# A zero-fill ahead of ScalarE's first transfer, and a ninth warm-up product, at the start of a hybrid encoder block

## The chip, the core and the metric

The kernel runs on one core of one Trainium2 chip. The metric is the device time of the whole program in microseconds, taken as the median of several runs. The core has a matrix engine (TensorE, called PE in the profile), three engines that work on tiles (VectorE or DVE, ScalarE or ACT, GpSimd or POOL) and SyncE (SP), which here only issues transfers. All transfers run on the same 16 DMA engines, whichever engine issues them.

## The reference, cut to what matters

One encoder block on 256 tokens of width 2048 in float32. What the change touches is only the very beginning, the first norm and the first projection:

```python
u = rmsnorm(h, norm_mix_g[l])
z = u @ w_in[l]
b_a, c_a, v_a, q, k, v, gl_a, gl_b = jnp.split(z, SPLIT_POINTS, axis=-1)
```

After it come a short gated convolution, a windowed attention, two gates, a mixing product, a second norm, a wide feed-forward pair of products with a convolution, and a last norm.

## The kernel before

**How a product is made.** Activations lie transposed, with the width on the partitions in 16 chunks (KT) of 128 rows and the 256 tokens in the columns. Every float32 product is split in two: the weight tile has a high part (`whi`, made by a cast on ACT, L175) and a low part (`wlo`, weight minus high part, on DVE, L186), and the activation tile holds its high and low part side by side in 512 columns (`xs`). One "pair" on PE is then a product of `whi` with 512 columns (L214) and one of `wlo` with 256 columns (L215). The whole program is a stream of such pairs, drawn from the list `chunks` in `run`. Three helpers run ahead of PE for each chunk: `fetch` issues the transfer, `high` makes `whi`, `low` makes `wlo`. All of it is emitted in an order written out by hand, and each engine works through its own instructions in that order.

**The first sixteen chunks.** They are "wide": chunk k holds row block k of the activations x (256 columns) beside row block k of six weight tiles (768 columns), and gives six pairs, one for each of the six jobs in `first`. For them `fetch`, `high` and `low` call `pre_x` at stages 0 to 3. `pre_x` also makes `xs` for chunk k from x and the norm's weight: for k below 3 both parts on DVE (L343 high, L344 low), later the high part on ACT (L336); and it squares x on ACT (L340).

**Chunk 0 is loaded differently.** The arrays for chunk 0 and the x of chunk 1 lie in one array `head`. Two transfers fetch it: SP's first (L319) brings the tile `hd`, 264 KB (the norm's weight, x of chunk 0, and weight blocks 0 and 1), and ACT's first (L320) brings the tile `hb`, 384 KB (weight blocks 2 to 5 of chunk 0, and x of chunk 1). SP then goes on with the wide transfers of chunks 1 to 15 (L326) on its own queue: the first is 384 KB, since its x came with `hb`, and the others are 512 KB. For chunks 0 to 2 the parts are made in two pieces, blocks 0 and 1 and then blocks 2 to 5 (`pieces`), so pairs 0 and 1 of chunk 0 rest on `hd` alone and pairs 2 to 5 on `hb`; chunk 1's `xs` rests on `hb` too.

**Before all that.** DVE fills `ones` (L302) and `eps` (L303), and PE multiplies `ones` by `ones` eight times into a bank that nobody reads (L308, `warm`). ACT's instructions begin with the issue of `hb`'s transfer; the load of its function table comes next, and then the casts.

Of the kernel before, what the change touches and what calls it, by code (L numbers as in the profile page):

```python
# [51 lines left out]
def hybrid_block_kernel(ctx: ExitStack, tc: tile.TileContext, head, wide, xT, w_in, w_oa, w_o, w_mix, w_up, w_dn, vec, cst, out):  # L52
    nc = tc.nc
# [245 lines left out]
    hb = p1.tile([P, WIDE, P], F32, tag="hb", name="hb")  # L299


    nc.vector.memset(ones, 1.0 / D)  # L302
    nc.vector.memset(eps, EPS)  # L303
    xs = cpool.tile([P, KT, 2 * T], F32R, tag="A", name="xs")

    warm = aps.tile([P, 2 * T], F32, tag="tp", name="warm")
    for _ in range(8):
        nc.tensor.matmul(warm[:, 0:P], ones, ones, start=True, stop=True)  # L308
    sq1 = cpool.tile([P, KT, T], F32, tag="B", name="sq1")

# [560 lines left out]
```

## Time and profile before

| what | us |
|---|---|
| median of 3 runs | 1334.39 (1333.92 to 1334.44) |
| the profiled execution, its own time | 1334.16 |
| span of its trace, first to last instruction | 1332.4 |
| PE busy in it | 1321.9 |
| PE's first pair starts at | 5.55 |

All times in the rows below are counted from the start of the span. A line of the timeline gives start, busy time, engine, line of the kernel, operation, and the tile written and read; the bracket at its end gives the idle time of the engine before it and what ended it. ACTq and SPq are the moments at which these engines issue a transfer. PEld is the loading of weights, which overlaps the products. One float32 product of `warm` shows as two records.

### The profile page before, as it was taken

The page shows a single profiled execution, that of the slowest core. Times are in us where ns is not written, and L with a number is a line of the kernel's source. Part 1 is how long each engine was busy: PE and PEld are TensorE (multiplying, and loading weights), DVE is VectorE, ACT ScalarE, POOL GpSimd, SP SyncE. Part 2 cuts the span into 40 slices and gives each one's busy share as a digit, 9 for nine tenths or more (in the row PEclk, how much of TensorE's full clock was granted, in tenths as well). Part 3 has the DMA queues.
Part 4 walks back from the last instruction along what each step waited for, and adds up shares of the span by engine and source line. Part 5 has one row for each costly group of instructions (what it writes and reads, how often), then busy time and mean ns, then how long its engine had stood idle before and what let it go on. Part 6 is the DMA issues. An engine that isn't in the chain of part 4 may idle for free.

```text
span 1332.4 us, 20489 instructions
## 1 busy us (share of the span) xinstructions
PE 1321.9 (99%) x7691; PEld 1162.7 (87%) x7691; DVE 955.4 (72%) x1507; ACT 722.4 (54%) x1151; POOL 71.1 (5%) x66
## 2 busy tenths in 40 slices
PE   9999999999999999999999999999999999999997
PEld 8888888888888888888888888888888888888886
DVE  6988777655557887668888888888888865445444
ACT  7666675555555545446555555555555544444442
POOL 0000000000000003330000000000000001111211
PEclk9999999999999999999999999999999999999999
DMA  8786545555555546547555555555555557666663
GB/s 289 245 240 203 205 159 168 180 190 189 191 190 190 190 145 235 191 139 239 190 189 190 190 190 190 190 190 190 190 189 191 174 151 234 195 187 181 197 192 103
DMA packets 76676, 255.54 MB, mean 192 GB/s; under 512 B 8864, under 2 KB 9248, under 8 KB 76576
## 3 DMA queue, kind: packets, MB, share of 16 engines
q1 hardware_dynamic: 76144, 253.44, 58.5%
q8 instruction: 60, 0.98, 0.3%
q10 hardware_dynamic: 432, 0.79, 0.2%
q14 instruction: 40, 0.33, 0.1%
HBM read 248.16 MB, written 2.10 MB: 188 GB/s over the span
## 4 chain that ended last, share of the span: by engine, by line
PE 99%; DVE 0%; DMA 0%; ACT 0%; POOLq 0%; issue 0%; DVEq 0%; ACTq 0%
PE ps L214 63%; PE ps L215 33%; PE av L490 1%; PE ptp L477 1%; PE s L447 0%; PE s L448 0%; DMA hd<-in_head_dram 0%; PE more L693 0%; POOLq L866 0%; DVE y L735 0%; DVE r L727 0%; DVE x L700 0%; ACT whi L175 0%; PE nps L258 0%; ACT ln L717 0%
## 5 line engine op out<-in xcount | busy, mean ns | idle before, releaser
L186 DVE TENSOR_TENSOR wlo<-raw,whi 128x1024 fp32r<-128x1024 f32 (+3 forms) x493 | 567.7, 1153 | 316.6 <-PE ps L215 223.4
L175 ACT CAST whi<-raw 128x1024 fp32r<-128x1024 f32 (+3 forms) x493 | 488.3, 992 | 328.5 <-PE ps L214 189.9
L214 PE MATMUL ps<-hs,whi 128*128 128x512 f32 x1408 | 488.4, 391 | 0.0
L215 PE MATMUL ps<-hs,wlo 128*128 128x256 f32 x1408 | 393.6, 280 | 0.0
L214 PE MATMUL ps<-xs,whi 128*128 128x512 f32 x1088 | 377.5, 395 | 0.7 <-ACT whi L175 0.7
L214 PEld LDWEIGHTS ps<-hs,whi 128*128 128x128 f32 x1408 | 263.1, 187 | 57.6
L215 PE MATMUL ps<-xs,wlo 128*128 128x256 f32 x1088 | 295.9, 281 | 0.0
L215 PEld LDWEIGHTS ps<-hs,wlo 128*128 128x128 f32 x1408 | 266.1, 189 | 0.4
L214 PEld LDWEIGHTS ps<-xs,whi 128*128 128x128 f32 x1088 | 200.7, 188 | 41.8 <-ACT whi L175 1.0
L215 PEld LDWEIGHTS ps<-xs,wlo 128*128 128x128 f32 x1088 | 206.4, 190 | 5.5
L244 ACT COPY evb<-ps 128x256 f32<-128x256 f32 x188 | 69.7, 372 | 199.3 <-PE ps L215 192.4
L214 PE MATMUL ps<-actC,whi 128*128 128x512 f32 x420 | 146.2, 391 | 0.0
L215 PE MATMUL ps<-actC,wlo 128*128 128x256 f32 x448 | 124.4, 280 | 0.0
L214 PEld LDWEIGHTS ps<-actC,whi 128*128 128x128 f32 x420 | 78.5, 187 | 17.2
L214 PE MATMUL ps<-ms,whi 128*128 128x512 f32 x256 | 88.8, 391 | 0.0
L214 PE MATMUL ps<-ya_att,whi 128*128 128x512 f32 x256 | 88.8, 391 | 0.0
L215 PEld LDWEIGHTS ps<-actC,wlo 128*128 128x128 f32 x448 | 84.8, 189 | 0.0
L214 PE MATMUL ps<-actA,whi 128*128 128x512 f32 x240 | 83.8, 391 | 0.0
L248 DVE TENSOR_TENSOR evt<-ps,evb 128x256 f32<-128x256 f32 x178 | 74.5, 418 | 0.7 <-ACT evb L244 0.7
L215 PE MATMUL ps<-ya_att,wlo 128*128 128x256 f32 x256 | 71.7, 280 | 0.0
L215 PE MATMUL ps<-ms,wlo 128*128 128x256 f32 x256 | 71.7, 280 | 0.0
L215 PE MATMUL ps<-actA,wlo 128*128 128x256 f32 x256 | 70.9, 280 | 0.0
(143 smaller groups left out, 1049.8 us busy)
## 6 DMA issues: line engine op xcount, KB each, us to landing
raw<-in_w_up_dram SPq DMA_DIRECT2D x170, 512.0 KB, 3.8
raw<-in_w_in_dram SPq DMA_DIRECT2D x124, 512.0 KB, 3.8
raw<-in_w_dn_dram SPq DMA_DIRECT2D x70, 512.0 KB, 4.3
raw<-in_w_mix_dram SPq DMA_DIRECT2D x26, 512.0 KB, 3.7
raw<-in_w_dn_dram SPq DMA_DIRECT2D x36, 256.0 KB, 2.7
raw<-in_w_oa_dram SPq DMA_DIRECT2D x16, 512.0 KB, 3.3
raw<-in_w_o_dram SPq DMA_DIRECT2D x16, 512.0 KB, 3.4
raw<-in_wide_dram SPq DMA_DIRECT2D x14, 512.0 KB, 5.4
```

The source lines that it names most:

```text
L175: nc.scalar.copy(his[c][:, a:b, :], raws[c](a, b))
L186: nc.vector.tensor_tensor(los[c][:, a:b, :], raw(a, b), his[c][:, a:b, :], op=ALU.subtract)
L214: lambda: nc.tensor.matmul(both, hi[:, i, :], moving, start=k == 0, stop=last and turned),
L215: lambda: nc.tensor.matmul(ps[:, 0:T], lo[:, i, :], a[:, 0:T], start=False, stop=last and not turned),
L244: nc.scalar.copy(b, ps[:, T : 2 * T])
L248: nc.vector.tensor_tensor(dst, ps[:, 0:T], b, op=ALU.add)
L477: nc.tensor.transpose(tp[:, b, n * P : (n + 1) * P], p[:, n, b * P : (b + 1) * P], ident)
L490: nc.tensor.matmul(o[64 * e : 64 * e + 64, 0:T], vtok[:, b, v0 : v0 + HD], pT[e][:, b, :], start=b == 0, stop=b == 1)
```

## The change

DVE fills the tile `hb` with zeros, after `ones` and `eps`. ACT's transfer into `hb` (L320) writes the same tile later in the program's order, so it now waits for that fill. The loop of warm-up products runs nine times rather than eight. Nothing else is edited.

```diff
     nc.vector.memset(ones, 1.0 / D)
     nc.vector.memset(eps, EPS)
+
+    nc.vector.memset(hb, 0.0)
     xs = cpool.tile([P, KT, 2 * T], F32R, tag="A", name="xs")
 
     warm = aps.tile([P, 2 * T], F32, tag="tp", name="warm")
-    for _ in range(8):
+    for _ in range(9):
         nc.tensor.matmul(warm[:, 0:P], ones, ones, start=True, stop=True)
```

`hb` is 128 partitions by 768 float32 elements.

## Rows read from the trace of the kernel before

**Rows 1.** The page: the span, the busy time of each engine with its share of the span, and the shares of the engines in the chain that ended last.

```profile
span 1332.4 us, 20489 instructions
...
PE 1321.9 (99%) x7691; PEld 1162.7 (87%) x7691; DVE 955.4 (72%) x1507; ACT 722.4 (54%) x1151; POOL 71.1 (5%) x66
...
PE 99%; DVE 0%; DMA 0%; ACT 0%; POOLq 0%; issue 0%; DVEq 0%; ACTq 0%
```

**Rows 2.** The waits of PE over the whole span: who waited for whom, us in total, times, longest.

```profile
PE warm L308 <- DVE eps L303: 1.1, 1, 1.1
PE nps L715 <- ACT sq L714: 1.0, 1, 1.0
PE ps L214 <- ACT whi L175: 0.7, 1, 0.7
```

**Rows 3.** The timeline of PE alone, from the start of the span.

```profile
1.05 3.79 PE L308 MATMUL warm<-ones 128*128 128x128 f32 x16 [1.05 <-DVE eps L303]
5.55 0.76 PE L214 MATMUL ps<-xs,whi 128*128 128x512 f32 x1 [0.72 <-ACT whi L175]
6.12 0.41 PE L215 MATMUL ps<-xs,wlo 128*128 128x256 f32 x1
6.33 0.63 PE L214 MATMUL ps<-xs,whi 128*128 128x512 f32 x1
...
6.97 0.63 PE L214 MATMUL ps<-xs,whi 128*128 128x512 f32 x1
7.40 0.41 PE L215 MATMUL ps<-xs,wlo 128*128 128x256 f32 x1
...
9.53 0.54 PE L214 MATMUL ps<-xs,whi 128*128 128x512 f32 x1
...
10.02 0.39 PE L214 MATMUL ps<-xs,whi 128*128 128x512 f32 x1
...
11.43 0.40 PE L214 MATMUL ps<-xs,whi 128*128 128x512 f32 x1
...
11.79 0.40 PE L214 MATMUL ps<-xs,whi 128*128 128x512 f32 x1
```

**Rows 4.** The timeline of all engines in the same stretch: the first issues of ACT and SP, and the work of ACT and DVE up to chunk 2.

```profile
0.73 0.41 ACTq L320 DMA_DIRECT2D hb<-in_head_dram  x1
0.74 0.38 SPq L319 DMA_DIRECT2D hd<-in_head_dram  x1
0.83 0.17 DVE L302 MEMSET ones<- 128x128 f32 x1 [0.83 <-PEq L860]
0.95 0.06 DVE L303 MEMSET eps<- 128x1 f32 x1
...
1.17 1.28 ACT L175 ACT_TABLE_LOAD   x1 [1.17 <-PEq L860]
...
4.54 0.41 ACT L175 CAST whi<-hd 128x256 fp32r<-128x256 f32 x1 [2.08 <-DMA hd<-in_head_dram]
4.54 0.35 DVE L343 TENSOR_SCALAR xs<-hd 128x256 fp32r<-128x256 f32 x1 [3.53 <-DMA hd<-in_head_dram]
4.85 0.61 ACT L175 CAST whi<-hb 128x512 fp32r<-128x512 f32 x1
4.92 0.48 DVE L344 SCALAR_TENSOR_TENSOR xs<-hd,xs 128x256 fp32r<-128x256 f32 x1
...
5.66 0.68 DVE L186 TENSOR_TENSOR wlo<-hb,whi 128x512 fp32r<-128x512 f32 x1
5.69 0.93 ACT L175 CAST whi<-raw 128x256 fp32r<-128x256 f32 x2 [0.23 <-DMA raw<-in_wide_dram]
...
7.51 0.93 ACT L175 CAST whi<-raw 128x256 fp32r<-128x256 f32 x2 [0.57 <-DMA raw<-in_wide_dram]
...
8.78 1.02 DVE L186 TENSOR_TENSOR wlo<-raw,whi 128x256 fp32r<-128x256 f32 x2
...
10.11 0.95 DVE L186 TENSOR_TENSOR wlo<-raw,whi 128x768 fp32r<-128x768 f32 x1
```

**Rows 5.** The transfers by line over the span: engine that issues, times, KB each, median us from issue to landing.

```profile
raw<-in_w_up_dram SPq DMA_DIRECT2D x12, 256.0 KB, 2.6
...
hb<-in_head_dram ACTq DMA_DIRECT2D x1, 384.0 KB, 4.0
raw<-in_wide_dram SPq DMA_DIRECT2D x1, 384.0 KB, 4.5
hd<-in_head_dram SPq DMA_DIRECT2D x1, 264.0 KB, 3.8
```

**Rows 6.** Windows: start and end, length, busy time and count of PE, PEld, DVE, ACT and POOL, the PEclk column, the mean busy share of the 16 DMA engines, and GB/s moved.

```profile
1.70:2.50 0.80, 0.80 (x6) 0.80 (x5) 0.00 (x0) 0.76 (x1) 0.00 (x0) 1.00 0.81 177
2.50:3.00 0.50, 0.50 (x4) 0.50 (x4) 0.00 (x0) 0.00 (x0) 0.00 (x0) 1.00 0.96 349
3.00:4.00 1.00, 1.00 (x7) 1.00 (x7) 0.00 (x0) 0.00 (x0) 0.00 (x0) 1.00 1.02 384
4.00:5.00 1.00, 0.84 (x4) 0.54 (x3) 0.43 (x2) 0.47 (x2) 0.00 (x0) 1.00 0.99 363
```

**Rows 7.** Groups of DVE's instructions in the first 40 us, different shapes kept apart: count, busy us and mean ns of one.

```profile
L186 DVE TENSOR_TENSOR wlo<-raw,whi 128x768 fp32r<-128x768 f32 x13 | 12.4, 958 | 6.5 <-ACT xs L336 4.9 <-issue 1.0 <-PE ps L215 0.6
...
L186 DVE TENSOR_TENSOR wlo<-raw,whi 128x256 fp32r<-128x256 f32 x2 | 0.8, 419 | 0.0
```

## The prediction

> **What bounds the kernel now.** Read the page first: PE is busy for 1321.9 of 1332.4 us, and the chain that ended last is PE for 99% [rows 1]. Then PE's waits: in the whole span it waits three times, 1.1 us before the first warm-up product, 0.7 us before the first pair and 1.0 us in the finale [rows 2]; what is left of the 10.5 us in which PE is not busy lies after its last product. So nothing but PE's own stream matters, and an edit at the start can give back only what the start loses. Third, PE's timeline from 0 [rows 3]: warm-up from 1.05 to 4.84, idle for 0.72, first pair at 5.55. The pairs then come 0.64 us apart (6.33, 6.97, up to 9.53), and from 10.02 on 0.353 apart ((11.43 - 10.02)/4). A pair is 768 columns, and 768 in 0.64 us is 1.2 a ns: the early pairs run at the clock's lower level, 1.2 GHz, the later ones near the upper. The PEclk column says 1.00 in the early windows too [rows 6], so it holds no reading there and the pace is what is to be trusted. From 9.53 to 10.02 is 0.49; x us at the slow pace and the rest at the fast one make one pair if x/0.64 + (0.49 - x)/0.353 = 1, so x = 0.31: the clock rises at 9.84. **The start loses two things**: 5.5 us before the first pair, and 0.29 us (0.64 - 0.353) on each of some seven slow pairs. My marker for the sum is the start of chunk 2's first pair, 11.79 [rows 3], after which the stream is gapless at the fast pace.
>
> **What sets 5.55.** `hd` is issued at 0.74 and lands after 3.8 us, so at 4.51; then come the cast of its weights and the two parts of its x (DVE 4.54 and 4.92, the second done at 5.40), and PE starts [rows 4, 5]. PE's wait is put down to a cast, but the cast of `hb` ends at 5.46 and the low part of x at 5.40, too near to tell them apart by that view; the code decides, since pairs 0 and 1 use `hd` alone. From landing to first pair are 1.04 us. `hb` is issued at the same moment and lands at 4.73.
>
> **The change, step by step.**
>
> *The fill.* `ones`, 128 elements a partition, takes 0.165 us, and `eps`, one element, 0.06 [rows 4]: (0.165 - 0.06)/127 is 0.83 ns an element. DVE's subtractions give (958 - 419)/512 = 1.05 ns [rows 7]. The fill of 768 elements is then 0.165 plus 640 times either, 0.70 to 0.84 us; I take 0.8, from 1.0 to 1.8. DVE has nothing to do until `hd` lands, so this time costs nothing on DVE itself.
>
> *ACT's wait.* `hb` goes out at about 1.84 (PE started 0.04 after `eps` ended), 1.1 later than now. Queued behind it on ACT is the table load (1.28 us from 1.17), which moves to about 2.27 and ends at 3.55. The first cast needs it; I put `hd`'s landing at 3.5, so the cover is just used up, at a cost of 0.05 for a cast that is not the last thing awaited. SP's queue has no wait added.
>
> *`hd` alone.* Between 1.7 and 3.0 the 16 engines move 0.14 + 0.17 MB, between 3 and 4 another 0.38 [rows 6]. `hd` is 0.27 MB: with nothing beside it, it is through at about 2.9, not 4. The landing is told later than the bytes: `hb` and `hd` together, 0.66 MB, are through at 3.9 and land by 4.73; I allow 0.6 to 0.8 and take 3.5. Bounds: 3.34 (a 256 KB transfer lands 2.6 us after its issue [rows 5]) and 4.51, no gain. The wide transfers on SP's queue stay behind `hd`, as now.
>
> *`hb` late.* By the time it moves, chunk 1's 384 KB is under way too. 264 + 384 + 384 KB are 1.06 MB, which the windows of rows 6 reach at 5.0; landing at 5.6 by the same allowance. Bounds: 1.84 + 3.2 = 5.05 (between the 256 KB row's 2.6 and `hb`'s own 4.0 in company) and 1.84 + 4.5 = 6.3 (chunk 1's 384 KB behind others [rows 5]). I take 5.6, the value from the bytes. Its cast (0.61) ends at 6.24, the subtraction `wlo<-hb` (0.68) then at 6.94, and pair 2's low product can start at 6.99. Now it starts at 7.40 [rows 3].
>
> *The ninth product.* Sixteen records take 3.79 us, the last one overlapping; two more make 0.43. PE is free for a pair at 4.63 now and at 5.06 then. With `hd` at 3.5 the first pair could start at 4.54, so PE starts at **5.06** and the idle 0.72 is gone. Seen alone, the ninth product costs 0.43 of the gain of 0.92 on the start.
>
> *The sum, with the clock left aside.* Pairs at 5.06 and 5.70, pair 2's high product at 6.34 (its cast is done at 6.24), its low product due at 6.77 but ready at 6.99: a stall of 0.22. Pair 3 at 7.20. At the slow pace chunk 0 then ends at 7.20 + 3 x 0.64 = 9.12. If the clock rises at 9.84 as now, 1.12 pairs of chunk 1 are done slowly and 4.88 fast: 9.84 + 1.72 = 11.56 against 11.79, a gain of 0.23.
>
> *The clock.* What the engine did before it rose: it ran without a gap from 5.55 to 9.84, idled 0.72 before that, and had worked from 1.05 to 4.84 with no rise [rows 3]. With the change the idle stretch is gone, work goes on from 1.05, and only the stall of 0.22 near 6.8 breaks it. I expect the rise between 5.06 and 9.84 and take the middle, 7.4. Then pair 3 is 0.31 done at 7.4, the 2.69 pairs left of chunk 0 take 0.95, chunk 1 takes 6 x 0.353 = 2.12, and chunk 2 starts at **10.47, a gain of 1.3**. Any rise earlier than 7.2 gives little more, because `hb` gates pair 2: at best pair 3 at 7.11 and chunk 2 at 10.29, a gain of 1.5.
>
> *What is late next.* DVE's whole backlog moves with `wlo<-hb`, from 5.66 to 6.26, by 0.6: chunk 2's subtractions (8.78, 1.02 long) end at 10.4, chunk 3's (10.11, 0.95 long) at 11.7 [rows 4]; PE wants them from 10.5 and 12.6 on, so they hold, with 0.1 to spare for chunk 2, in which the second piece is needed two pairs later. ACT's casts of chunk 2 wait for a transfer at 7.51 both ways, since the bytes ahead of it are the same.
>
> The profiled execution took 1334.16, 1.8 outside its span, and lies 0.23 under the median. 1334.16 - 1.3 + 0.23 gives 1333.1.
>
> **The rivals.**
>
> *The clock does not follow the gap.* The rise stays where it was and the gain is the 0.23 above: 1334.2. For it: the rise came 4.3 us after the idle stretch ended, and no row shows what PE would have got without it. Against it: 3.79 us of unbroken work, then idle time, then 4.29 us of unbroken work, and only in the last a rise. The Trainium skill ("TensorE: Matmul & The Clock Gate", Part 1: The HAM clock gate) says that the monitor runs freely and does not begin with the kernel, so that the number of slow products differs between runs of one kernel. By that rule the gain would scatter between runs; that the three runs lie within 0.52 us speaks for less scatter than that.
>
> *`hb` comes too late, and the kernel is slower.* The place is pair 2. The point from which it decides: its low product starts 1.39 after `hb` lands (0.03 + 0.61 + 0.02 + 0.68 + 0.05), which is later than today's 7.40 if `hb` lands after 6.0. At the bound of 6.3, pair 2's high product waits from 6.34 to 7.0 and its low one starts at 7.69. That idle time is as long as today's and ends 2.14 later; if the rise moves with it, to 11.98, chunk 0 ends at 9.82, 3.4 pairs of chunk 1 are slow and 2.6 fast, and chunk 2 starts at 12.9: 1.1 slower, 1335.5. For it: chunk 1's 384 KB took 4.5 us, and the engines are full from 2.5 on (0.96 to 1.02 [rows 6]). The Trainium skill ("DMA: Bandwidth & Descriptors", Issuing engines are not separate DMA queues) speaks against the change in the same way: transfers of both queues share the 16 engines, so what `hd` gains `hb` loses. Against it: only one transfer's bytes, not three, lie in `hb`'s way.
>
> *The head's load is not faster.* If `hd` alone lands at 4.51 still, pair 0 starts at 5.55 as now, `hb`'s lateness is hidden (pair 2's low product is due at 7.26), and nothing changes: 1334.4. For it: the first packets need time whatever else runs (177 GB/s up to 2.5). Against it: the byte count and the 256 KB row.
>
> **How the numbers follow.** Forecast 0.58 (1332.3 to 1333.6: from `hb` at its early bound, a gain of 2.05, to a rise not before 8.2), the clock unmoved 0.23, no faster head 0.07, slower 0.12. The range takes in the first three and the noise of runs: 1332.2 to 1334.8. A measurement of this kernel can tell about 0.2%, 2.7 us, from no change. No case reaches that: the largest gain is 2.05 and the largest loss 1.1. What is left for either side is what no row shows: faster 0.03, slower 0.02, the same 0.95.
>
> **What would show it.** In the profile after: a MEMSET of `hb` of 0.7 to 0.84 us on DVE; ACT's issue near 1.84 and the table load near 2.27; the first cast near 3.55; warm-up with 18 records to 5.27; the first pair near 5.06 with no idle time before it; a short wait of PE for `wlo<-hb` near 6.8; 0.353 between pairs well before 9.8; and the start of chunk 2 near 10.5. The prediction is wrong in its main step if the pairs still come 0.64 apart up to about 9.5, and wrong in sign if PE waits for `hb` past 7.4.

## The result, and the profile after

The changed kernel takes **1338.14 us** (median of 9 runs, 1336.76 to 1339.57) against 1333.92 for the kernel before (9 runs, 1332.38 to 1334.46): a ratio of 1.0037, 95% interval 1.0028 to 1.0045. It is slower, by more than the 2.7 us that the prediction called the least a measurement can tell. The profiled execution took 1337.80 with a span of 1336.0, against 1334.16 and 1332.4 before.

The first place to look is PE's waits. Before, 0.7 us stood ahead of the first pair [rows 2]; now there is one wait of 4.1:

```profile
PE ps L214 <- ACT whi L175: 4.1, 1, 4.1
```

PE's timeline tells where it lies. It answers to [rows 3]:

```profile
1.05 3.62 PE L310 MATMUL warm<-ones 128*128 128x128 f32 x18 [1.05 <-DVE ones L302]
4.50 0.47 PE L214 MATMUL ps<-xs,whi 128*128 128x512 f32 x1
...
5.19 0.28 PE L215 MATMUL ps<-xs,wlo 128*128 128x256 f32 x1
9.57 0.80 PE L214 MATMUL ps<-xs,whi 128*128 128x512 f32 x1 [4.10 <-ACT whi L175]
10.30 0.58 PE L215 MATMUL ps<-xs,wlo 128*128 128x256 f32 x1
10.68 0.63 PE L214 MATMUL ps<-xs,whi 128*128 128x512 f32 x1
...
11.32 0.63 PE L214 MATMUL ps<-xs,whi 128*128 128x512 f32 x1
...
14.35 0.39 PE L214 MATMUL ps<-xs,whi 128*128 128x512 f32 x1
...
15.41 0.40 PE L214 MATMUL ps<-xs,whi 128*128 128x512 f32 x1
```

The first pair starts a whole microsecond earlier (4.50 against 5.55), and pairs 0 and 1 run fast. Pair 2 then starts at 9.57, and the pairs are 0.64 apart again (10.68, 11.32) until about 14. Chunk 2 starts at 15.41 against 11.79: 3.62 later. From there to the end of the span are 1320.6 us in both traces, so that is the whole difference of 3.6 between the spans.

The cause of the wait is in the timeline of DVE, ACT and SP (it answers to [rows 4]), and in the transfers issued in the first 1.85 us (KB each, us from issue to landing; the 512 and 384 KB of `raw` are chunks 2 and 1):

```profile
1.11 0.70 DVE L305 MEMSET hb<- 128x768 f32 x1
1.17 2.42 SPq L328 DMA_DIRECT2D raw<-in_wide_dram  x5
1.84 0.39 ACTq L322 DMA_DIRECT2D hb<-in_head_dram  x1
2.26 1.28 ACT L175 ACT_TABLE_LOAD   x1 [2.26 <-DVE hb L305]
3.48 0.35 DVE L345 TENSOR_SCALAR xs<-hd 128x256 fp32r<-128x256 f32 x1 [1.67 <-DMA hd<-in_head_dram]
3.55 0.40 ACT L175 CAST whi<-hd 128x256 fp32r<-128x256 f32 x1
...
8.90 0.62 ACT L175 CAST whi<-hb 128x512 fp32r<-128x512 f32 x1 [4.95 <-DMA hb<-in_head_dram]
```

```profile
raw<-in_wide_dram SPq DMA_DIRECT2D x1, 512.0 KB, 7.0
raw<-in_wide_dram SPq DMA_DIRECT2D x1, 384.0 KB, 3.6
hb<-in_head_dram ACTq DMA_DIRECT2D x1, 384.0 KB, 7.0
hd<-in_head_dram SPq DMA_DIRECT2D x1, 264.0 KB, 2.7
```

`hd` lands at 0.74 + 2.7, about 3.45. `hb` goes out at 1.84 and takes 7.0 us where it took 4.0 [rows 5]; it lands at 8.87, just before its cast. What happens to it is told by the queues: q1 is SP's, q10 ACT's. The columns are packets, MB, and share of the 16 engines' time. First the span's first 5.1 us, then its first 6.15:

```profile
q1 hardware_dynamic: 379, 1.04, 62.5%
```

```profile
q1 hardware_dynamic: 420, 1.16, 58.0%
q10 hardware_dynamic: 65, 0.20, 9.5%
```

In 5.1 us SP's queue has moved 1.04 MB, and ACT's not one packet, 3.3 us after its issue. When half of `hb`'s 0.39 MB has begun, SP has moved 1.16 MB. Ahead of `hb` in time of issue were `hd` (0.74), chunk 1 (1.17) and chunk 2 (1.64): 264 + 384 + 512 KB, 1.19 MB. Chunk 2 itself lands only at 8.64, 7.0 us after its issue, though SP had moved 1.16 of the 1.19 MB by 6.15; the experiment on the tail comes back to that.

The clock, too, is told by windows. The columns are those of [rows 6]; PEclk is the third from the end:

```profile
7.40:9.50 2.10, 0.00 (x0) 0.00 (x0) 0.00 (x0) 0.60 (x2) 0.00 (x0) 0.50 1.02 415
9.57:13.88 4.31, 4.31 (x12) 3.39 (x13) 4.24 (x10) 4.31 (x11) 0.00 (x0) 0.50 0.49 156
14.20:18.00 3.80, 3.80 (x23) 3.30 (x23) 2.72 (x5) 2.82 (x7) 0.00 (x0) 1.00 0.88 274
```

PE had stopped at 5.47; from 7.4 the granted clock is 0.50, the level of 1.2 GHz, and it stays there through PE's first 4.3 us of work.

### The profile page after: what moved, and what is told of

It reads as the page before. It is cut to its first block, busy times and chain, and to the rows that moved or that the text cites. A ratio compares the mean times of both kernels' runs of the same rounds, so it can differ in the third digit from the quotient of the medians.

```text
span 1336.0 us, 20494 instructions
## 1 busy us (share of the span) xinstructions
PE 1322.1 (99%) x7693; PEld 1162.5 (87%) x7693; DVE 956.6 (72%) x1508; ACT 722.5 (54%) x1151; POOL 70.9 (5%) x66
## 4 chain that ended last, share of the span: by engine, by line
PE 98%; DMA 1%; DVE 0%; ACT 0%; POOLq 0%; issue 0%; DVEq 0%; ACTq 0%
PE ps L214 63%; PE ps L215 33%; PE av L492 1%; PE ptp L479 1%; DMA hb<-in_head_dram 1%; PE s L449 0%; PE s L450 0%; PE more L695 0%; POOLq L868 0%; DVE y L737 0%; DVE r L729 0%; DVE x L702 0%; PE nps L258 0%; ACT ln L719 0%; PE nps L717 0%
```

## The experiments

The theory after the result: `hb` waits for every transfer issued before it, on whichever queue; the fill moves its issue behind those of chunks 1 and 2, and that is the loss. The main rivals: the ninth product; the wait or ACT's queue as such; the lateness of the issue by itself; and the prediction's own picture, in which the two queues share the engines evenly. Medians below stand beside a ratio to the kernel before with its interval. Diffs are against the changed kernel where nothing else is said.

**The two halves of the change.** `fill_only` has the fill and eight products:

```diff
-    for _ in range(9):
+    for _ in range(8):
```

> The fill of hb alone, with eight warm-up products as before. Theory (the loss comes from hb's transfer, which goes out at 1.84 behind chunks 1 and 2 and lands at 8.9): the same loss as the whole change, 1338 us within 1, first packets of hb near 5.1, landing near 8.9, PE idle some 4 us before pair 2. Rival (the ninth product costs, or the wait matters only together with it): well under 1337.

1337.34 us, ratio 1.0028 (1.0016 to 1.0039); `hb` again out at 1.84 and 7.0 us on its way, and a wait of PE of 3.5 us. `nine_only` is the kernel before with the loop raised to nine:

```diff
-    for _ in range(8):
+    for _ in range(9):
```

> The ninth warm-up product alone, no fill, hb issued at 0.73 as before. Theory (it only fills part of the idle time before the first pair, which stays near 5.5 because hd still lands at 4.5): no loss, 1332.0 to 1334.5, the idle time before the first pair falls from 0.72 to about 0.3. Rival (the ninth product carries the loss): over 1336.

1332.49, ratio 0.9995 (0.9986 to 1.0003). So the loss is the fill's. The idle stretch shrinks to 0.29 as expected, and in this execution the pairs are fast from the first one on:

```profile
5.55 0.47 PE L214 MATMUL ps<-xs,whi 128*128 128x512 f32 x1 [0.29 <-ACT whi L175]
...
6.02 0.40 PE L214 MATMUL ps<-xs,whi 128*128 128x512 f32 x1
...
6.37 0.40 PE L214 MATMUL ps<-xs,whi 128*128 128x512 f32 x1
```

**The place in the order of issue, moved by the length of the fill.** `fill_short_first`: one column, ahead of chunk 1's issue.

```diff
+    nc.vector.memset(hb[:, 0:1, 0:1], 0.0)
     nc.vector.memset(ones, 1.0 / D)
     nc.vector.memset(eps, EPS)
-
-    nc.vector.memset(hb, 0.0)
```

> Nine products; the fill covers one column of hb and stands first on DVE, so ACT's transfer still waits for a fill but goes out at about 0.95, before SP's issue of chunk 1 at 1.17. Theory (hb waits behind what was issued before it): only hd is ahead, first packets of hb near 2.2, landing at 4.6 to 5.1, hd at 3.6 to 4.4; 1331.8 to 1333.5. Rival (the wait on ACT's first transfer, or the order head first, is what costs): hb lands after 6, over 1335.

1332.11, ratio 0.9992 (0.9983 to 1.0001): `hb` out at 0.90, 3.8 us on its way, and no loss although ACT's transfer waits for a fill and `hd` goes first. `fill_third`: two of six blocks.

```diff
-    nc.vector.memset(hb, 0.0)
+    nc.vector.memset(hb[:, 0:2, :], 0.0)
```

> The whole change, but the fill covers a third of hb (256 elements a partition), so hb's issue falls at about 1.42, between SP's issues of chunk 1 (1.17) and chunk 2 (1.64). Theory (behind what was issued before): first packets only when chunk 1 is nearly through, at 3.6 to 4.2, landing at 5.7 to 6.5, PE idle for 0.5 to 1.5 us before pair 2; 1333 to 1335.5. Rival (the prediction's own: the queues share the engines evenly from 1.3 us after the issue): first packets at 2.7, landing near 5.2, no idle time worth telling; 1332 to 1333.

1333.08, ratio 1.0001 (0.9992 to 1.0010). The issue fell at 1.31, just after chunk 1's at 1.18; it took 4.6 us and landed at 5.93, in the theory's range. The idle time of 0.5 to 1.5 us was not there: pair 1 ended at 6.54 and pair 2 started at 6.62. The time lies where the two ranges meet, so it decides nothing; the landing and the queues (below) do. `fill_longer`: four blocks filled a second time.

```diff
     nc.vector.memset(hb, 0.0)
+    nc.vector.memset(hb[:, 0:4, :], 0.0)
```

> The whole change, and four of hb's six blocks are filled a second time, so hb's issue falls at about 2.28, after SP's issue of chunk 3 (2.11) and before chunk 4 (2.58): 0.44 us later than in the change. Theory (behind what was issued before): 512 KB more ahead of it, first packets near 6.3 to 6.9, landing at 9.9 to 11, 1.0 to 2.0 us later than the change in all: 1339 to 1340.5. Rival (the lateness of the issue itself counts, one for one): landing 0.4 later than 8.9, 1338.6.

1339.01, ratio 1.0045 (1.0031 to 1.0059). The issue fell at 2.50, later than planned, and landing took 7.2 us, to 9.7: a little under the theory's range in the landing, and at its lower edge in the time. By the landing alone the theory can't be told from the rival here (0.66 later in issue, 0.8 later in landing). The queues tell them apart. In each kernel, up to the moment at which half of `hb`'s packets have begun (65 to 68 on q10): the first 3.45 us of `fill_short_first`, the first 4.4 of `fill_third`, and the first 7.6 of `fill_longer`.

```profile
q1 hardware_dynamic: 144, 0.27, 30.5%
q10 hardware_dynamic: 67, 0.21, 15.1%
```

```profile
q1 hardware_dynamic: 285, 0.66, 46.5%
q10 hardware_dynamic: 68, 0.21, 12.4%
```

```profile
q1 hardware_dynamic: 541, 1.62, 65.2%
q10 hardware_dynamic: 64, 0.20, 6.5%
```

| kernel | `hb` issued at, us | issued before it, MB | moved on SP's queue when half of `hb`'s packets had begun, MB | landing after, us | median, us |
|---|---|---|---|---|---|
| `fill_short_first` | 0.90 | 0.27 | 0.27 | 3.8 | 1332.11 |
| `fill_third` | 1.31 | 0.66 | 0.66 | 4.6 | 1333.08 |
| the change | 1.84 | 1.19 | 1.16 | 7.0 | 1338.14 |
| `fill_longer` | 2.50 | 1.71 | 1.62 | 7.2 | 1339.01 |

Column four follows column three over a factor of six. For what was issued before `hb` that is an order of issue over both queues, and no even sharing. In the change, even sharing from 1.3 us after the issue would have begun at 3.1, when SP had moved 0.37 MB, and half of `hb` (0.2 MB) would have been under way beside another 0.2 MB of SP's, at about 0.57 and not at 1.16. Where two transfers go out within 0.01 us of each other, the queues do share evenly; in the kernel before, with `hb` out at 0.73 and `hd` at 0.74, half of `hb` has begun at 3.2 us, and by then:

```profile
q1 hardware_dynamic: 91, 0.19, 24.0%
q10 hardware_dynamic: 65, 0.20, 17.2%
```

**The same place without a fill, a wait or ACT's queue.** `hb_on_sp` leaves the fill out and issues `hb` on SP, second:

```diff
-    nc.vector.memset(hb, 0.0)
...
-                nc.scalar.dma_start(hb, by_block(head[:, HEAD:]))
+                nc.sync.dma_start(hb, by_block(head[:, HEAD:]))
```

> Nine products, no fill; hb's transfer is issued on SP's queue right after hd's, so its place in the order of issue is fixed as second, and ACT's queue carries no load at the start. Theory (order of issue decides): hd lands at 3.5, hb's packets follow hd's and hb lands at 4.6 to 5.1, PE starts at 4.5 to 5.1 and has at most 0.5 us of stall before pair 2; 1331 to 1333. Rival (hb's lateness after the change is a matter of hd going first at all): hb lands after 6 and the time is over 1335.

1332.74, ratio 0.9996 (0.9987 to 1.0005); `hb` out at 1.17, landing after 3.7, PE without a wait before pair 2. `hb_third_on_sp` issues it on SP after chunk 2, where the change puts it:

```diff
-    nc.vector.memset(hb, 0.0)
...
-                nc.scalar.dma_start(hb, by_block(head[:, HEAD:]))
...
             nc.sync.dma_start(raw[:, x0:, :], wide[k, :, x0:, :])
+            if k == 2:
+                nc.sync.dma_start(hb, by_block(head[:, HEAD:]))
```

> Nine products, no fill, no wait; hb's transfer goes out on SP's own queue, after chunks 1 and 2 and before chunk 3 (issue near 2.1, the place in the order of issue that it has in the change). Theory (its place in the order costs the time, not ACT's queue and not the wait): first packets near 5, all of the 264 + 384 + 512 + 384 KB through by 6.8 to 7.1 since nothing issued later shares with it, landing at 7.2 to 7.9, PE idle 1.5 to 2.5 us before pair 2: 1335 to 1337. Rival (only a transfer on ACT's queue is held back): landing under 6, 1332 to 1334.

1337.40, ratio 1.0031 (1.0020 to 1.0042). Landing at 7.7 as expected, the time 0.4 over the range. With no fill, no wait and an idle ACT queue the kernel loses nearly as much as the change (1.0031 against 1.0037, and the intervals overlap): the place in the order is enough. The trace is of the fastest of the seven runs (1336.40), so in the others `hb` may have landed later. Chunk 2, the transfer of `hb`, and the first pair that needs it:

```profile
raw<-in_wide_dram SPq DMA_DIRECT2D x1, 512.0 KB, 5.1
hb<-in_head_dram SPq DMA_DIRECT2D x1, 384.0 KB, 5.6
```

```profile
8.41 0.50 PE L214 MATMUL ps<-xs,whi 128*128 128x512 f32 x1 [2.22 <-ACT whi L175]
```

**The late issue kept, the transfers ahead taken away.** `sp_after_hb` makes SP's chunk 1 wait for a fill too, so that only `hd` goes ahead of `hb`:

```diff
             x0 = 2 if k == 1 else 0
+            if k == 1:
+                nc.vector.memset(raw[:, 2:3, 0:1], 0.0)
```

> The whole change, and one column of chunk 1's tile is filled on DVE after hb's fill, so that SP's transfers of chunk 1 to 5 go out after hb's issue at 1.84 too, and hb's issue is as late as in the change. Theory (order of issue): hb has only hd ahead of it, first packets at about 3.1, landing at 4.6 to 5.3, no long idle time; 1331 to 1334. Rival (an issue at 1.84 is too late by itself, or ACT's queue gets nothing while SP's queue holds chunks 1 to 5): hb lands after 7, over 1336.

1336.01, ratio 1.0019 (1.0010 to 1.0028). Between the two expectations. The issue is at 1.85, as late as in the change, and landing is at 6.9, not 8.9: so with those transfers out of its way it lands 2 us earlier at the same moment of issue. But about half of the loss stays (1.0019 of 1.0037), and the landing is not 4.6 to 5.3 either. The windows show a part of the reason:

```profile
2.50:3.00 0.50, 0.50 (x4) 0.50 (x4) 0.00 (x0) 0.50 (x1) 0.00 (x0) 1.00 0.81 313
3.00:4.00 1.00, 1.00 (x7) 1.00 (x7) 0.49 (x2) 0.96 (x2) 0.00 (x0) 1.00 0.63 140
4.00:5.00 1.00, 1.00 (x7) 1.00 (x6) 0.68 (x2) 0.00 (x0) 0.00 (x0) 1.00 0.91 270
```

With nothing queued behind `hd`, the engines run dry near 3 and start slowly a second time (140 GB/s between 3 and 4, as 177 at the very start [rows 6]), and chunk 1, issued within 0.01 us of `hb`, shares with it (it landed at 6.8, `hb` at 6.9). I had counted neither; how much each costs was not measured apart.

**What holds the tail.** In the change, `hb`'s packets begin at 5.1 and it lands at 8.87. At the 350 GB/s that the engines moved from 5.1 to 8.6, 384 KB would take 1.1 us. `hold_chunk3` keeps chunk 3 back until `hb` has landed:

```diff
             x0 = 2 if k == 1 else 0
+            if k == 3:
+                nc.gpsimd.tensor_copy(raw[:, 0:1, 0:1], hb[:, 0:1, 0:1])
```

> The whole change, and SP's transfer of chunk 3, with all behind it, waits until hb has landed (GpSimd copies one element of hb into chunk 3's tile first). Theory (hb has chunks 1 and 2 ahead of it and then shares the engines with chunk 3, which costs the last 1 to 1.5 us): first packets of hb still near 5, landing at 6.9 to 7.7 and not 8.9, pair 2 at 7.6 to 8.5; 1335 to 1337. Rival (the engines are slow for hb whatever runs beside it): landing at 8.5 to 9, 1338.

1337.05, ratio 1.0028 (1.0018 to 1.0038). Landing after 6.6, at 8.4: sharing with chunk 3 costs some 0.45, not the 1 to 1.5 I expected, and the landing is nearer to the rival's 8.5 than to the theory's range; the time, just past the upper end of the range, does not mend that. The windows show the engines' mean busy share (the last column but one) falling while `hb` is still not in:

```profile
6.00:7.00 1.00, 0.54 (x2) 0.03 (x1) 0.00 (x0) 0.00 (x0) 0.00 (x0) 1.00 0.49 196
7.00:8.00 1.00, 0.00 (x0) 0.00 (x0) 0.00 (x0) 0.00 (x0) 0.00 (x0) 1.00 0.18 72
```

A share of 0.18 is on average about three of 16 engines at work: it looks as if a few engines lag by more than a microsecond behind the others. The tail is not `hb`'s alone. Chunk 2 lands 7.0 us after its issue in the change, 0.2 before `hb`, and 6.6 here, with chunk 3 held back; with `hb` behind it on SP's own queue it took 5.1. So the order of issue held at the start of `hb`, while at its end `hb` and chunk 2 finished nearly together. Whether two queues at once make the tail, and why engines lag, is open.

**Idle time and clock apart.** `fillers` puts 18 products of `ones` by `ones` (FILLERS) into PE's wait:

```diff
+FILLERS = 18
...
+                if c == 0 and i == 1:
+                    for _ in range(FILLERS):
+                        nc.tensor.matmul(box["warm"][:, 0:P], ones, ones, start=True, stop=True)
...
     warm = aps.tile([P, 2 * T], F32, tag="tp", name="warm")
+    box["warm"] = warm
```

> The whole change, and 18 more products of ones by ones between pair 1 and pair 2 of chunk 0, in PE's idle time while hb is on its way (their result is read by nobody). Theory (the loss is two things, idle time and the clock that falls in it): hb lands as late as in the change, but the clock does not fall, the pairs from 9.6 on come 0.353 apart, and some 6 to 7 slow pairs at 0.29 are saved: 1335.8 to 1336.8. Rival (the clock's fall costs nothing, because chunk 1's and 2's parts are not ready for fast pairs): 1338 as the change.

1336.38, ratio 1.0027 (1.0017 to 1.0038). In this execution pairs 0 and 1 were still slow (4.92 to 5.70), so the clock rose among the fillers, and with no idle time it did not fall: the pairs after the wait come 0.35 apart:

```profile
10.57 0.48 PE L215 MATMUL ps<-xs,whi 128*128 128x512 f32 x1
...
11.02 0.40 PE L215 MATMUL ps<-xs,whi 128*128 128x512 f32 x1
...
11.37 0.40 PE L215 MATMUL ps<-xs,whi 128*128 128x512 f32 x1
...
14.20 0.40 PE L215 MATMUL ps<-xs,whi 128*128 128x512 f32 x1
```

From pair 2 to chunk 2 are 3.63 us (10.57 to 14.20) against 5.84 in the change (9.57 to 15.41). So 2.2 of the loss is the low clock together with the wait for `wlo` at pair 2, though the fillers, a little too many, give 1.0 of it back by putting off pair 2. By the medians the fillers save 1.8, by the spans of the two traces 0.8; the trace is of the slowest of the seven runs (1337.01).

**The ninth product where `hb` is not late.** `short_first_eight` is `fill_short_first` with eight products (diff against that kernel).

```diff
-    for _ in range(9):
+    for _ in range(8):
```

> The one-column fill that stands first on DVE, with eight products: hb out at 0.90, ahead of chunk 1. It tells what the ninth product is worth where hb is not late. Theory (an idle stretch of 0.3 us at most before the first pair, hd landing near 3.8): the first pair at 4.7 to 4.9, the time within 0.5 us of the same kernel with nine, 1331.7 to 1332.8. Rival (the ninth product keeps the clock): the time falls into two groups as the kernel before does, the upper near 1334.

1332.25 (11 runs, 1331.82 to 1333.77), ratio 0.9989 (0.9981 to 0.9998): the same as with nine, faster than the changed kernel by some 6 us, and just below the kernel before, whose runs fall into two groups (last section); its lower group beside them, 1332.1 to 1332.5, lies where these runs lie. Ten of the eleven are below 1332.6, so the rival's two groups are not there. The first pair started at 4.98, a little after the expected 4.7 to 4.9.

## Why the prediction was wrong

- **What bounds the kernel**: right. Only the start of PE's stream changed; the 3.62 us at chunk 2 are the whole difference of the spans.
- **The fill and ACT's issue**: right. 0.70 us (bounds 0.70 to 0.84), issue at 1.84, table load 2.26 to 3.54.
- **`hd` alone**: right. Landing after 2.7 us, at 3.45 (3.5 predicted).
- **`hb` late**: this step failed. "264 + 384 + 384 KB ... landing at 5.6", with 6.3 as the upper bound; it landed at 8.87. The term that was put at nothing without a reason is chunk 2: its 512 KB are not in that sum, which counts the bytes that an even sharing of the engines between the queues would move. The runs show an order of issue in its place: by 1.84 SP had issued chunk 2 as well (at 1.64), and most of the 1.19 MB went ahead of `hb`: SP had moved 1.04 MB before its first packet, and 1.16 when half of it had begun (1.11 in `hold_chunk3`, without chunk 3). The row of chunk 1's 4.5 us was no upper bound, since chunk 1 had nothing but the head ahead of it; so the largest loss of 1.1 was none either. Of the 4.1 us between the landings before and after (4.73 and 8.87), `hb_third_on_sp`, landing at 7.7, shows 3.0 with the place in the order alone. The rest is the tail: sharing with chunk 3 (0.45), and what looks like a few lagging engines, which stays open.
- **From landing to product**: right. 1.39 after the landing was the sum; 8.87 + 1.39 = 10.26, measured 10.30.
- **The ninth product**: it costs nothing that shows (0.9995 alone, and with a short fill the same with eight as with nine). It does hold the first pair where the clock stays low: in the traces of `fillers`, `hold_chunk3`, `fill_longer` and `fill_third` 18 records take 4.21 us and the first pair starts at 4.91 or 4.92 (5.06 predicted), against 4.56 with eight in `fill_only`. There `hb` decides all the same. That the first pair came at 4.50 in the profile after looks like the chance of that execution: the last warm-up products ran at the upper pace (18 records in 3.62 us, where 16 took 3.79 [rows 3]).
- **The clock**: the rise came earlier, but before the first pair and so outside the forecast's 5.06 to 9.84, and then was lost again. That the removed idle time brought it is not shown: in `fillers` and `hold_chunk3`, with the same start, pairs 0 and 1 are slow. That the idle time of 4.1 us would bring the low level back was not in the sum, because the idle time was not.
- **The rivals**: the slow one was the right mechanism at the right place, given 0.12. Its price, 1.1 us, was worked out at a landing of 6.3. Put the measured landing and the measured rise of about 14.1 into the same sum: pair 3 at 10.47, chunk 0 done at 12.39, 2.7 slow and 3.3 fast pairs of chunk 1, chunk 2 at 15.3 against the measured 15.41. The argument against it, "only one transfer's bytes, not three, lie in `hb`'s way", is the false sentence: behind `hd` it was chunk 1 and most of chunk 2, and chunk 3 shared. That chunk 2 goes out before 1.84 could be read off SP's timeline, which I had not put beside the time of ACT's issue. A slip in the forecast's inner range changed nothing: a rise at 8.2 gives chunk 2 at 10.83 by the prediction's own sum, so 1333.4 and not 1333.6.
- **The Trainium skill** ("DMA: Bandwidth & Descriptors", Issuing engines are not separate DMA queues) says that transfers of all queues run on the same engines and interleave. I took the interleaving as even. The trace agrees that the queues interleave once both have begun: from 5.1 to 6.15 SP's queue moved 0.12 MB and ACT's 0.20. But 1.04 MB of SP's queue passed before ACT's first packet.

Shown: the place in the order of issue is enough to cost nearly all of the time, with or without the fill, the wait, ACT's queue and the ninth product. Not shown: where in the machinery the order is kept, what makes the tail, and how the loss that stays in `sp_after_hb` divides.

## What to carry to other kernels

A wait ahead of a transfer can cost more than its own length, because what other queues issue in it goes ahead: 1.1 us of wait here cost 3.0 us in the transfer's own time besides. Before a transfer is moved, list what every queue issues between its old and its new moment, and count those bytes as going ahead in full. If one transfer must go ahead of another, the smallest delay that turns their order will do (0.17 us here), or the same queue.

## What was not expected of the hardware

- **Order over queues.** A transfer on ACT's queue, issued 0.2 us after SP's third, sent its first packet 3.3 us after its issue, when SP had moved 1.04 MB; issued 0.16 us after SP's first, it landed after 3.8 us. Issued within 0.01 us of each other, the two queues shared evenly (0.19 and 0.20 MB by 3.2 us).
- **A second slow start.** After the engines had run dry, they moved 140 GB/s in the next microsecond and 270 in the one after, with 768 KB and more queued (`sp_after_hb`).
- **The kernel before falls into two groups.** In the 29 runs beside the first experiments, 10 lie between 1332.1 and 1332.8 and 16 between 1333.8 and 1334.7; the trace the prediction rests on (1334.16) is of the upper group. Against the lower group alone the change loses more than 5 us. With nine products alone 10 of 11 lie under 1333.0. The clock's rise would explain it: pairs become fast at 9.84 in the profiled execution of the kernel before, and from 5.55 in that of `nine_only` (1332.29). The Trainium skill ("TensorE: Matmul & The Clock Gate", Part 1: The HAM clock gate) says that the number of slow products differs between runs of one kernel, because the monitor does not begin with it; that agrees, but with one profile per kernel it is not shown that the clock makes the groups.
